# Queries made one group ahead, mixer sums and rotations on VectorE, and other rates for a background gather, in a two-layer diffusion backbone on one core

## Chip, cores and metric

One core of one Trainium2 chip. The metric is device time in microseconds (us) of one execution of the whole program: all work is one launch, with the inputs in the chip's main memory.

## What is computed

Two layers over 512 latent tokens and 256 context tokens of width 1024, all in float32. A layer first mixes tokens by three gated branches, then applies a retrieval of single-neuron experts:

```python
h = rms_norm(x) * (1 + scale1) + shift1
x += gate1 * W_out( sum_i sigmoid(h W_gate_i) * (branch_i(h) W_br_i) )
     # branches: windowed attention (8 heads, 2 kv heads, axial rotation, sinks, context keys),
     #           multi-scale pooling, chunked spatial gating
h = rms_norm(x) * (1 + scale2) + shift2
x += gate2 * peer(h)      # 8 heads, top 16 of 128*128 experts each: gelu(h . u_e) * softmax gate * v_e
```

The context tokens pass through layer 0 only (mixer and experts); layer 1 needs just their keys and values.

## The kernel before

The program runs in stages: the mixer of the context (0 to about 267 us), the mixer of the latent tokens in layer 0 (to about 785), the experts of layer 0 (`peer`, to about 2390), the latent mixer of layer 1 (to about 2835), the experts of layer 1 (to the end).

**Matmuls** are made in three passes (`mm3`, L217 to L223): weights and inputs are split into a rounded part and a remainder (`whi`, `wlo`), so every weight tile costs one load of 512 KB, one ScalarE copy (L189), one VectorE subtraction (L190) and 24 matmuls. `Weights.take` hands out such a tile in a fixed list order; each take is also a tick of `Background` (L48 to L79). A background job has a rate, and at every tick it makes that many steps.

**The experts of the latent tokens** are computed densely: for each of 128 tiles of u (L920 to L948) and then 128 tiles of v (L1060 to L1108), one take each. The selected gates are made by the job `front` on VectorE during the first 95 tiles.

**The 256 context tokens** find their experts' rows by gathering: for each of 2 blocks, 128 rows of u and then 128 rows of v per token. A step of the job `gather` (L804 to L829) issues one indirect transfer of 512 KB on POOL's queue (L801) into one of four buffers, two steps ahead, and consumes one on VectorE (L818 for u, L823 for v). These VectorE instructions keep their program order. 512 steps and 6 empty ones start in the layer-0 latent mixer (`gather_experts`, L1186) and end in the mixer of layer 1. The rates: 2.2 per take from the keys on (21 takes), 2.0 from the last branch on (16 takes) and in the output projection (8 takes), then by `peer`'s tuple 1.8 for the first 40 tiles of u, 1.4 for the next 55, 1.8 for the last 32; over v the rest is spread as `steps left / (128 + 8)` (L1038).

**A mixer** (`mixer`, L377) takes its weights in the order of `WS` (L394): spatial gating, keys, then per head group g its queries and two tiles of each of two output channels of the pooling branch, then the attention branch, then the output projection. `branch` (L482) makes, per output channel block o, a gate (`pj` to `th`, L491), the branch's product (`pb`), their product (`mt`, L501), and adds it to the sum `mg` (L502); the last branch also splits the sum into `mr` (L504) for the output projection (`pw_`, L673). The sum runs on POOL except for the last two blocks of the last branch. `rope` (L535) rotates keys and queries: a shuffle on VectorE, a multiplication by sin on POOL (L538), and two VectorE instructions.

The attention loop (L639) makes, per group, the queries (L640 to L645), then for each block b of 128 tokens the scores of both kv heads (`pc`, two buffers; maximum on VectorE L585, exponential on ScalarE L587) and the weighing of the block before (`weigh`: transposes L600, copies L602, products `po` L610). In group 0 two blocks of the pooling branch are made before the scores of b = 0; in groups 1 to 3 one before b = 0 and one before b = nb / 2.

Tile names: `g` gathered rows, `dots` and `hN` their results, `kT`, `qT`, `qs` keys and queries, `rs` the rotated copy, `wm` a job of layer 1's mixer that computes modulation vectors.

The framework orders each engine's instructions itself by a priority list, so moving a line in the code moves instructions on several engines.

Of the kernel before, what the change touches and what calls it, by code (L numbers as in the profile page):

```python
# [14 lines left out]
ALU = mybir.AluOpType  # L15
# [4 lines left out]
P = 128  # L20
# [62 lines left out]
def tile_backbone(ctx: ExitStack, tc: tile.TileContext, A, out):  # L83
# [5 lines left out]
    bg = Background()  # L89
# [287 lines left out]
    def mixer(l, x, r, lat, ps, start=None, settle=None, clear=None, after_attention=None, finish=None):  # L377
# [3 lines left out]
        with ExitStack() as es:  # L381
# [100 lines left out]
            def branch(br, wn, nk):  # L482
# [5 lines left out]
                for o in range(NCH):  # L488
# [8 lines left out]
                    if br == 2:  # L497
                        dve.scalar_tensor_tensor(mg[:, o], th, 1.0, pb, op0=ALU.add, op1=ALU.mult)
                    else:
                        t = pl.tile([P, T], F32, name="mt", tag="tt", bufs=3)  # L500
                        dve.scalar_tensor_tensor(t, th, 1.0, pb, op0=ALU.add, op1=ALU.mult)  # L501
                        (pool if br == 1 or o < 6 else dve).tensor_tensor(mg[:, o], mg[:, o], t, op=ALU.add)  # L502
                        if br == 0:
                            split(mr[0][o], mr[1][o], mg[:, o])  # L504
# [30 lines left out]
            def rope(t):  # L535
                s = pl.tile([P, T], F32, name="rs", tag="rs", bufs=2)
                dve.stream_shuffle(s, t, SHUF)
                pool.tensor_tensor(s, s, sin, op=ALU.mult)  # L538
                dve.tensor_tensor(t, t, cos, op=ALU.mult)
# [98 lines left out]
            last, ended = [], []  # L638
            for g in range(4):  # L639
                q = at.tile([P, T], F32, name="qT", tag="qT", bufs=2)  # L640
# [3 lines left out]
                qs2 = at.tile([P, 2, T], F32R, name="qs2", tag="qs2", bufs=2)  # L644
                split(qs2[:, 0], qs2[:, 1], q)  # L645
                finish_block()
                po = ps.tile([P, T], F32, name="po", tag="po", bufs=1)
                st = at.tile([P, 2, 2, nb], F32, name="st", tag="st", bufs=2)
                for b in range(nb):
                    for _ in range(2 * (b == 0) if g == 0 else b % (nb // 2) == 0):  # L650
                        next(second)
                    found = scores(qs2, st, g, b)
                    finish_group()
                    finish_block()
                    last.append((po, st, g, *found))
            finish_block()
            finish_group()
# [528 lines left out]
    def gather_experts():  # L1186
        bg.drain(jobs.pop())
        right.close()
        g4[0] = ctx.enter_context(tc.tile_pool(name="g4", bufs=1, side="right"))
        jobs.append(bg.add(gather(cblocks, 6), 2.2, 4 * P + 6))  # L1190

    def faster(pl, ps):
        jobs[0][1] = 2.0

    r = mixer(0, xT, rx[0], True, mps, start=find_experts, clear=gather_experts, after_attention=faster)
    eh.close()
    with tc.manual_schedule(engines={mybir.EngineType.Pool}):
        r = peer(0, r, (1.8, 1.4, 1.8, -8))

# [117 lines left out]
```

## Time and profile before

| | us |
|---|---|
| median of 3 runs (4096.03 to 4104.95) | 4099.12 |
| the profiled execution's own time | 4101.82 |
| its span, first to last instruction | 4100.0 |

PE is busy for 95% of the span, VectorE (DVE) for 77%, ScalarE (ACT) for 37%, POOL for 29%. A busy share averages over stages with different limits; a row of a window view gives the share of one stage.

### The profile page before, as it was taken

What the parts mean: (1) busy time and instruction counts of PE and PEld (TensorE: products, weight loads), DVE (VectorE), ACT (ScalarE), POOL (GpSimd) and SP (SyncE); (2) the same over time, 40 slices, a digit from 0 to 9 for tenths busy, and PEclk for the clock granted to TensorE, in tenths of its full rate; (3) what the DMA queues carried; (4) which work ended last, traced back from release to release, by engine and by line L of the source; (5) the groups of instructions that cost most, each with busy time, mean ns of one, the idle gap of its engine ahead of it and who ended that gap; (6) DMA issues with size and microseconds to landing.
All of it is one profiled execution on the core that took longest, in us unless ns stands there. A gap on an engine that the chain in (4) does not pass through costs nothing. (4 is left out here: it accounts for less than half of the span.)

```text
span 4100.0 us, 59061 instructions
## 1 busy us (share of the span) xinstructions
PE 3906.6 (95%) x21737; PEld 3391.9 (83%) x21737; DVE 3146.7 (77%) x6154; ACT 1498.7 (37%) x2320; POOL 1183.0 (29%) x942
## 2 busy tenths in 40 slices
PE   7999898899999999999999979999999999999998
PEld 5788776678778888788888867777889999999998
DVE  4569876799998876677778875645889986788887
ACT  3553343323344433222222233443234443333333
POOL 1111244411643324343333331110002224423331
PEclk9999999899999999999999989999999999999999
DMA  7753456655998998889999854323348999989996
GB/s 282 260 172 111 147 173 212 226 189 184 325 317 309 318 308 275 296 299 358 350 344 358 318 173 140 119 89 105 118 153 295 334 332 323 341 312 353 364 358 224
DMA packets 366099, 1051.86 MB, mean 257 GB/s; under 512 B 38384, under 2 KB 131312, under 8 KB 361200
## 3 DMA queue, kind: packets, MB, share of 16 engines
q1 hardware_dynamic: 170928, 544.18, 37.6%
q0 software_dynamic: 110592, 402.70, 28.5%
q10 hardware_dynamic: 84288, 101.20, 7.0%
q8 instruction: 170, 2.79, 0.3%
q14 instruction: 121, 0.99, 0.1%
HBM read 943.61 MB, written 104.33 MB: 256 GB/s over the span
## 5 line engine op out<-in xcount | busy, mean ns | idle before, releaser
L189 ACT CAST whi<-wraw 128x1024 fp32r<-128x1024 f32 (+2 forms) x756 | 752.6, 997 | 1672.2 <-issue 596.0
L190 DVE TENSOR_TENSOR wlo<-wraw,whi 128x1024 fp32r<-128x1024 f32 (+2 forms) x756 | 876.3, 1161 | 571.1 <-ACT whi L189 465.4
L801 POOL DMA_INDIRECT g<-in_u_dram,idx x384 | 500.9, 1304 | 1228.4 <-DVE dots L818 816.7
L801 POOL DMA_INDIRECT g<-in_v_dram,idx x384 | 511.8, 1333 | 913.3 <-DVE hN L823 845.5
L220 PE MATMUL pa<-h,whi 128*128 128x512 f32 (+1 forms) x2016 | 744.0, 369 | 2.5 <-ACT a L942 2.5
L1083 PE MATMUL acc<-ah,whi 128*128 128x512 f32 (+1 forms) x2048 | 740.4, 363 | 5.6 <-ACT ah L214 5.6
L1085 PE MATMUL acc<-ah,wlo 128*128 128x512 f32 (+1 forms) x2048 | 741.5, 362 | 0.0
L1084 PE MATMUL acc<-al,whi 128*128 128x512 f32 (+1 forms) x2048 | 741.4, 362 | 0.0
L221 PE MATMUL pa<-h,whi 128*128 128x512 f32 (+1 forms) x2016 | 734.4, 364 | 0.0
L818 DVE CUSTOM_DVE_ANT_0 g<-g,hN 128x1024 f32<-128x1024 f32 x384 | 466.2, 1236 | 50.5 <-DMA g<-in_u_dram,idx 50.4
L823 DVE SCALAR_TENSOR_TENSOR hN<-g,gate,hN 128x1024 f32<-128x1024 f32 x381 | 487.2, 1279 | 13.4 <-DMA g<-in_v_dram,idx 12.9
L223 PE MATMUL pa<-h,wlo 128*128 128x512 f32 (+1 forms) x2016 | 450.2, 364 | 2.9 <-DVE wlo L190 2.9
L1083 PEld LDWEIGHTS acc<-ah,whi 128*128 128x128 f32 x2048 | 384.7, 188 | 47.2 <-ACT ah L214 7.2
L1084 PEld LDWEIGHTS acc<-al,whi 128*128 128x128 f32 x2048 | 385.1, 188 | 40.4
L1085 PEld LDWEIGHTS acc<-ah,wlo 128*128 128x128 f32 x2048 | 385.0, 188 | 40.2
L220 PEld LDWEIGHTS pa<-h,whi 128*128 128x128 f32 x2016 | 381.1, 189 | 40.9 <-ACT a L942 2.8
L221 PEld LDWEIGHTS pa<-h,whi 128*128 128x128 f32 x2016 | 380.8, 189 | 38.2
L223 PEld LDWEIGHTS pa<-h,wlo 128*128 128x128 f32 x2016 | 368.5, 189 | 42.6 <-DVE wlo L190 3.2
L220 PE MATMUL pj<-h,whi 128*128 128x512 f32 (+1 forms) x792 | 288.9, 376 | 6.6 <-DVE nx L295 3.2
L221 PE MATMUL pj<-h,whi 128*128 128x512 f32 (+1 forms) x792 | 280.9, 366 | 1.3 <-POOL h L300 0.9
L942 ACT ACTIVATE a<-pa 128x512 f32<-128x512 f32 (+1 forms) x256 | 139.3, 546 | 271.1 <-PE pa L223 203.7
L220 PEld LDWEIGHTS pj<-h,whi 128*128 128x128 f32 x792 | 154.5, 195 | 46.8 <-issue 11.5
(527 smaller groups left out, 5428.2 us busy)
## 6 DMA issues: line engine op xcount, KB each, us to landing
wraw<-in_uT_dram SPq DMA_DIRECT2D x256, 512.0 KB, 5.3
wraw<-in_v_dram SPq DMA_DIRECT2D x256, 512.0 KB, 5.9
gd<-gs ACTq DMA_DIRECT2D x28, 2048.0 KB, 13.2
wraw<-in_winT_dram SPq DMA_DIRECT2D x100, 512.0 KB, 4.2
wm<-in_wmod_dram SPq DMA_DIRECT2D x64, 512.0 KB, 5.2
g<-gd SPq DMA_DIRECT2D x16, 2048.0 KB, 10.6
wraw<-in_wq_dram SPq DMA_DIRECT2D x48, 512.0 KB, 3.9
ad<-a ACTq DMA_DIRECT2D x96, 256.0 KB, 4.9
```

The costliest lines, as they stand in the source:

```text
L189: act.copy(hi, raw)
L190: dve.tensor_tensor(lo, raw, hi.bitcast(F32), op=ALU.subtract)
L220: pe.matmul(ps, wh[i], xh[i], start=i == 0, stop=False)
L221: pe.matmul(ps, wh[i], xl[i], start=False, stop=False)
L223: pe.matmul(ps, wl[i], xh[i], start=False, stop=i == n - 1)
L801: pool.indirect_dma_start(out=g, out_offset=None, in_=A[table], in_offset=bass.IndirectOffsetOnAxis(ap=idx, axis=0))
L818: ins = dve.tensor_tensor_reduce(out=g, in0=g, in1=hN, op0=ALU.mult, op1=ALU.add, scale=1.0, scalar=0.0, accum_out=dots[:, s:s + 1])
L823: ins = dve.scalar_tensor_tensor(hN, g, w, hN, op0=ALU.mult, op1=ALU.add)
L942: act.activation(a, pa[:, n_w:], AF.Gelu_apprx_tanh)
L1083: pe.matmul(acc[c], wh[:, s], ah, start=n == 0 and c % pair == 0, stop=False)
L1084: pe.matmul(acc[c], wh[:, s], al, start=False, stop=False)
L1085: pe.matmul(acc[c], wl[:, s], ah, start=False, stop=n == P - 1 and (c % pair == 1 or pair == 1 and not blocks))
```

## The change

Four edits. (1) The sums `mg` of all branches run on VectorE. (2) The sin product of `rope` runs on VectorE. (3) The queries of group g + 1 are made after the scores of block nb / 2 of group g, and group 0 has one block of the pooling branch before b = 0 and one before b = nb / 2, as the others. (4) The gather's rates fall from 2.2 to 1.0 and from 2.0 to 1.3 in the layer-0 mixer, and rise from 1.4 to 1.5 and from 1.8 to 2.3 in the second and third stretch of u.

```diff
-                        (pool if br == 1 or o < 6 else dve).tensor_tensor(mg[:, o], mg[:, o], t, op=ALU.add)
+                        dve.tensor_tensor(mg[:, o], mg[:, o], t, op=ALU.add)
...
                 dve.stream_shuffle(s, t, SHUF)
-                pool.tensor_tensor(s, s, sin, op=ALU.mult)
+                dve.tensor_tensor(s, s, sin, op=ALU.mult)
...
-            for g in range(4):
+            def queries():
                 q = at.tile([P, T], F32, name="qT", tag="qT", bufs=2)
                 act.mul(q, proj(ps, ws, hh, hl, T), 0.125)
                 if lat:
                     rope(q)
                 qs2 = at.tile([P, 2, T], F32R, name="qs2", tag="qs2", bufs=2)
                 split(qs2[:, 0], qs2[:, 1], q)
+                return qs2
+            coming = queries()
+            for g in range(4):
+                qs2 = coming
                 finish_block()
...
                 for b in range(nb):
-                    for _ in range(2 * (b == 0) if g == 0 else b % (nb // 2) == 0):
+                    if b % (nb // 2) == 0:
                         next(second)
                     found = scores(qs2, st, g, b)
                     finish_group()
                     finish_block()
                     last.append((po, st, g, *found))
+                    if b == nb // 2 and g < 3:
+                        coming = queries()
...
-        jobs.append(bg.add(gather(cblocks, 6), 2.2, 4 * P + 6))
+        jobs.append(bg.add(gather(cblocks, 6), 1.0, 4 * P + 6))
...
-        jobs[0][1] = 2.0
+        jobs[0][1] = 1.3
...
-        r = peer(0, r, (1.8, 1.4, 1.8, -8))
+        r = peer(0, r, (1.8, 1.5, 2.3, -8))
```

POOL in the last branch of the layer-0 latent mixer, before: `L801` issues an indirect transfer, `L502` is a sum.

```order
L801 DMA g_6732<-in_u_dram,idx 128x1024
L502 TENSOR_TENSOR mg<-mg,mt 128x512
L801 DMA g_6768<-in_u_dram,idx 128x1024
L801 DMA g_6771<-in_u_dram,idx 128x1024
L801 DMA g_6798<-in_u_dram,idx 128x1024
L801 DMA g_6801<-in_u_dram,idx 128x1024
L502 TENSOR_TENSOR mg<-mg,mt 128x512
L801 DMA g_6837<-in_u_dram,idx 128x1024
```

The same place of the changed kernel, where the indirect transfer is on line 809:

```order
L809 DMA g_6717<-in_u_dram,idx 128x1024
L809 DMA g_6753<-in_u_dram,idx 128x1024
L809 DMA g_6756<-in_u_dram,idx 128x1024
L809 DMA g_6783<-in_u_dram,idx 128x1024
L809 DMA g_6819<-in_u_dram,idx 128x1024
```

Four issues stood between two sums; now two or three fall to a channel block, and no sum stands among them.

VectorE in the layer-1 mixer, group 0, from the queries' remainder (`qs`) to the first score maxima (`mx<-pc`), before:

```order
L215 TENSOR_TENSOR qs_22680<-qT,qs_22680 128x512
L162 ISA wm,mod_80<-wm,silu,bm 128x1024
L162 ISA mod_80 128x1
L190 TENSOR_TENSOR wlo<-wraw,whi 128x1024
L501 SCALAR_TENSOR_TENSOR mt<-th,pb 128x512
L162 ISA wm,mod_80<-wm,silu,bm 128x1024
L162 ISA mod_80 128x1
L190 TENSOR_TENSOR wlo<-wraw,whi 128x256
...
L190 TENSOR_TENSOR wlo<-wraw,whi 128x1024
L501 SCALAR_TENSOR_TENSOR mt<-th,pb 128x512
L585 TENSOR_REDUCE mx<-pc 128x1 x2
```

And in the changed kernel:

```order
L215 TENSOR_TENSOR qs_22680<-qT,qs_22680 128x512
L162 ISA wm,mod_80<-wm,silu,bm 128x1024
L162 ISA mod_80 128x1
L501 SCALAR_TENSOR_TENSOR mt<-th,pb 128x512
L585 TENSOR_REDUCE mx<-pc 128x1
L502 TENSOR_TENSOR mg<-mg,mt 128x512
L586 TENSOR_TENSOR mx<-mx,nsk 128x1
L585 TENSOR_REDUCE mx<-pc 128x1
```

The second channel block of the pooling branch no longer stands ahead of the first maximum; a sum does.

VectorE in the same mixer at the end of group 0, changed kernel: the next group's rotation (`rs`, `qT`) among the maxima of the last block of scores. Before, it stood behind `L621` of this group.

```order
L537 STREAM_SHUFFLE rs<-qT 128x512
L585 TENSOR_REDUCE mx<-pc 128x1
L538 TENSOR_TENSOR rs<-rs,sin 128x512
L539 TENSOR_TENSOR qT<-qT,cos 128x512
L586 TENSOR_TENSOR mx<-mx,nsk 128x1
L585 TENSOR_REDUCE mx<-pc 128x1
L540 TENSOR_TENSOR qT<-qT,rs 128x512
L586 TENSOR_TENSOR mx<-mx,nsk 128x1
L215 TENSOR_TENSOR qs_22977<-qT,qs_22977 128x512
```

A maximum of the last block now waits behind up to three rotation instructions.

## Rows read from the trace of the kernel before

**Rows 1.** The page's head, its busy times, and the 40 slices of the span (102.5 us each): PE's and VectorE's busy tenths, the granted TensorE clock in tenths, and the data rate.

```profile
span 4100.0 us, 59061 instructions
PE 3906.6 (95%) x21737; PEld 3391.9 (83%) x21737; DVE 3146.7 (77%) x6154; ACT 1498.7 (37%) x2320; POOL 1183.0 (29%) x942
PE   7999898899999999999999979999999999999998
DVE  4569876799998876677778875645889986788887
PEclk9999999899999999999999989999999999999999
GB/s 282 260 172 111 147 173 212 226 189 184 325 317 309 318 308 275 296 299 358 350 344 358 318 173 140 119 89 105 118 153 295 334 332 323 341 312 353 364 358 224
```

**Rows 2.** The view of windows: stretch and its length in us, then the busy us (and instructions) of PE, of weight loads, of VectorE, ScalarE and POOL, the granted clock, the DMA share and GB/s. In order: attention of the layer-0 latent mixer, its last branch, the three stretches of u in layer 0, most of v in layer 0, attention of the layer-1 mixer, its last branch, and v in layer 1.

```profile
453.00:636.00 183.00, 163.60 (x1034) 130.45 (x1033) 133.50 (x229) 82.61 (x185) 73.18 (x56) 0.98 0.51 166
636.00:736.00 100.00, 76.66 (x298) 59.29 (x297) 62.05 (x97) 22.31 (x32) 54.15 (x38) 0.90 0.70 229
785.00:1118.00 333.00, 318.82 (x1587) 260.08 (x1586) 312.71 (x1084) 106.33 (x144) 107.26 (x67) 0.99 0.67 229
1118.00:1490.00 372.00, 369.81 (x2205) 303.90 (x2204) 323.94 (x420) 158.03 (x235) 141.02 (x85) 1.00 0.92 316
1490.00:1676.00 186.00, 185.31 (x830) 153.05 (x828) 108.83 (x129) 57.15 (x71) 71.86 (x57) 1.00 0.82 276
1800.00:2362.00 562.00, 562.00 (x2481) 465.35 (x2480) 448.74 (x536) 162.19 (x207) 192.85 (x168) 1.00 0.93 341
2532.00:2712.00 180.00, 166.01 (x1036) 132.79 (x1035) 114.97 (x199) 83.56 (x185) 23.23 (x13) 0.97 0.36 119
2712.00:2780.00 68.00, 68.00 (x297) 55.12 (x296) 28.16 (x36) 23.58 (x32) 9.76 (x6) 1.00 0.31 101
3700.00:4000.00 300.00, 300.00 (x1733) 300.00 (x1732) 250.50 (x299) 106.77 (x144) 95.50 (x80) 1.00 0.98 361
```

**Rows 3.** ScalarE's timeline (start us, length, instruction, idle before it and its releaser), the marks of both latent mixers: the keys, the first gate of the last branch, the first and the last of the eight squares that follow the output projection's channel blocks. Layer 0, then layer 1.

```profile
453.88 0.59 ACT L544 COPY kT<-pj 128x512 f32<-128x512 f32 x1 [0.76 <-PE pj L223]
636.72 0.60 ACT L491 ACTIVATE th<-pj 128x512 f32<-128x512 f32 x1 [0.76 <-PE pj L223]
736.31 0.63 ACT L253 ACTIVATE nsq<-xT 128x512 f32<-128x512 f32 x1 [3.11 <-DVE xT L674]
774.28 0.63 ACT L253 ACTIVATE nsq<-xT 128x512 f32<-128x512 f32 x1 [4.87 <-DVE xT L674]
...
2532.63 0.59 ACT L544 COPY kT<-pj 128x512 f32<-128x512 f32 x1 [0.76 <-PE pj L223]
2712.04 0.60 ACT L491 ACTIVATE th<-pj 128x512 f32<-128x512 f32 x1 [0.76 <-PE pj L223]
2780.01 0.63 ACT L253 ACTIVATE nsq<-xT 128x512 f32<-128x512 f32 x1 [1.55 <-DVE xT L674]
2817.93 0.63 ACT L253 ACTIVATE nsq<-xT 128x512 f32<-128x512 f32 x1 [4.87 <-DVE xT L674]
```

**Rows 4.** The view of waits, 650 to 785 us: engine and line waiting, what it waited for, us in total, times, the longest.

```profile
ACT mr L214 <- POOL mg L502: 42.7, 5, 10.9
DVE g L818 <- DMA g<-in_u_dram,idx: 32.3, 6, 7.1
PE pj L223 <- DVE wlo L190: 14.5, 5, 5.8
```

**Rows 5.** Groups of VectorE's and POOL's instructions by form in the last branch of layer 0's latent mixer, 636 to 736 us: count, busy us and mean ns, idle time before them and its releasers.

```profile
L818 DVE CUSTOM_DVE_ANT_0 g<-g,hN 128x1024 f32<-128x1024 f32 x31 | 37.8, 1254 | 32.3 <-DMA g<-in_u_dram,idx 32.3
L818 DVE DVE_READ_ACCUMULATOR2_ANT dots<- 128x1 f32 x31 | 2.5, 80 | 0.0
L502 DVE TENSOR_TENSOR mg<-mg,mt 128x512 f32<-128x512 f32 x2 | 1.4, 703 | 0.0
L801 POOL DMA_INDIRECT g<-in_u_dram,idx x32 | 46.8, 1464 | 54.3 <-DVE dots L818 49.4 <-issue 4.9
L502 POOL TENSOR_TENSOR mg<-mg,mt 128x512 f32<-128x512 f32 x6 | 8.1, 1358 | 1.7 <-DVE mt L501 1.6
```

**Rows 6.** DMA issues from 640 to 785 us: count and median us from issue to landing.

```profile
g<-in_u_dram,idx POOLq DMA_INDIRECT x42, 5.9
```

**Rows 7.** Waits of PE in the layer-1 mixer's attention (2532 to 2712 us).

```profile
PE pc L574 <- ACT s L587: 10.5, 4, 5.3
PE po L610 <- ACT sT L602: 1.9, 3, 1.5
```

**Rows 8.** The view of windows again, stretches of 6 us in the layer-1 mixer at the first scores of group 0 (two rows) and near that group's end.

```profile
2554.00:2560.00 6.00, 0.75 (x7) 0.54 (x5) 4.97 (x10) 3.27 (x6) 1.26 (x1) 0.85 0.90 302
2560.00:2566.00 6.00, 6.00 (x26) 5.85 (x26) 1.97 (x4) 2.90 (x9) 0.00 (x0) 0.58 0.10 35
2572.00:2578.00 6.00, 4.46 (x46) 3.47 (x44) 4.69 (x10) 3.15 (x9) 0.00 (x0) 1.00 0.11 34
```

**Rows 9.** One tile's instructions, the queries `qT`, over the whole span: count, min, median and max ns.

```profile
L539 DVE TENSOR_TENSOR qT<-qT,cos x8: 692/1764/1776, 463.8 to 2670.1; 128x512 f32<-128x512 f32 x8
```

**Rows 10.** Waits of PE in the context's mixer (0 to 267 us).

```profile
PE pc L574 <- ACT s L587: 2.9, 2, 2.3
```

**Rows 11.** The last stretch of u in layer 0 (1490 to 1676 us): the activations, one per tile of u, and the issues of the gather's transfers; count, min, median and max ns, first and last start.

```profile
L942 ACT ACTIVATE a<-pa x34: 592/598/603, 1494.8 to 1675.3; 128x512 f32<-128x512 f32 x34
L801 POOL DMA_INDIRECT g<-in_u_dram,idx x40: 933/941/1863, 1549.7 to 1667.2; - x40
```

## The prediction, on record before the changed kernel ran

> **What bounds the kernel now.** I read the page first [rows 1]: PE is busy for 3906.6 of 4100 us, so at most 193 us of idle time are to be had, and the tenths show where: the experts' stages stand at 9, the mixers (slices 1 to 8 and 24 to 27) at 7 to 9. Then the windows by stage [rows 2]. From 1118 to 2362 us PE waits for almost nothing (369.81 of 372, 185.31 of 186, 562 of 562), so no edit can gain there; it can only lose. From 636 to 736 us PE is busy for 76.66 of 100 us at a granted clock of 0.90, while the same code in layer 1 takes 68 us at 1.00 with PE full. In both attention stages PE idles: 183 - 163.6 = 19.4 us and 180 - 166 = 14.0 us.
>
> The marks on ScalarE give the stages their lengths [rows 3]. Last branch, from the first gate to the first square: 736.31 - 636.72 = 99.6 us in layer 0 against 2780.01 - 2712.04 = 68.0 in layer 1, which has no gather there. Keys to first gate: 182.8 against 179.4. The output projection, first square to last: 38.0 against 37.9, although layer 0 gathers two steps per take in it.
>
> So one stage loses 31.6 us to the gather. Its waits [rows 4] say how: VectorE stands 32.3 us waiting for gathered rows to land, PE 14.5 us for a `wlo` queued behind, ScalarE's `mr` 42.7 us for a sum on POOL. The groups of that stage [rows 5] close the account: VectorE's 62.05 busy us [rows 2] and its 32.3 us of waiting are 94.4 of the 99.6. VectorE sets the pace, and the rows that land late set VectorE's.
>
> **The change, part by part.** The sum is made against the profiled execution, 4101.8 us, which lies 2.7 us above the median of the runs.
>
> *Last branch of layer 0's mixer.* 16 takes at 1.3 make 20.8 steps where 2.0 made 32 (the rows show 31 in the window). Ten steps fewer free 10 x (1.254 + 0.080) = 13.3 us of VectorE; six sums moved there cost 6 x 0.703 = 4.2 [rows 5]. Its work becomes 62.05 - 13.3 + 4.2 = 53 us, under PE's 68. What matters is the landing. A buffer's round is an issue of 1.46, a landing of 5.9 [rows 6] and a use of 1.33: 8.7 us for four buffers. A channel block of two takes lasts 8.5 us at layer 1's pace; before, it asks for four rows, all buffers at once, and a sum of 1.36 us on POOL stands between the issues. After, it asks for 2.6, so a buffer has 13 us, and POOL's queue holds issues alone. If the waiting only shrank with the count (32.3 x 21 / 31 = 21.9), VectorE would need 75 us, a gain of 25; if the stage falls to PE's pace, 31.6; if all 32.3 us stayed, 85, a gain of 14. I take **28**, nearest to the output projection, which at 2.0 per take loses nothing [rows 3]. Ends: 14 and 32.
>
> *Attention, layer 1.* No gather runs there, so this is the order alone. The longest PE wait is 5.3 us for the exponentials of the first scores [rows 7]: VectorE has a whole pooling block in front of the first maximum. Behind it the clock stays low: 0.58 in the next 6 us and 0.85 in the wait itself [rows 8], that is 6 x 0.42 = 2.5 us of work at half of 2.4 GHz. With one block moved behind the scores of b = 1, the wait shrinks to about a maximum, an exponential and one sum, an estimated 1.5 us, and the clock need not fall: 3.8 + 2.5 = 6.3. The queries, 24 matmuls, now lie under the last block's softmax and cover the 1.5 us wait for `sT` near the end of group 0 [rows 7, 8]. Against that, the rotation stands among the maxima of the last block: up to three instructions of 0.7 (the minimum in [rows 9]), 2.1 us, covered by the transposes, products and the 5.5 us of the queries on PE; without that cover it would cost 2.1 us in three groups. I take **7**, ends -2 and 12 (of the 14 us idle and the 0.03 of 180 us that the clock lacks, some 19, a third must remain for softmax latencies).
>
> *Attention, layer 0.* The same 7, and the 3.4 us by which it is longer than layer 1's, since its steps fall from 46 to 21 in 21 takes: 25 x 1.33 = 33 us less on VectorE. I take **10**, ends 1 and 16.
>
> *Rotation and sums on VectorE elsewhere.* The multiplication by cos takes 0.692 at best and 1.764 in the median [rows 9]: beside POOL's multiplication it is held up by 1.07 us. So moving the product adds 0.69 us and takes away about as much. Attention holds 13 of these instructions, where VectorE is busy for 0.64 of layer 1's stage and 0.73 of layer 0's [rows 2]; I cost them at nothing, hidden by PE's matmuls, at the price of 13 x 0.7 = 9 us a mixer if VectorE were the bound.
>
> *Context mixer.* PE waits 2.9 us for exponentials [rows 10]; the order change can take part of it. Take **1**, ends -1 and 3. Its sums add 14 short instructions to a VectorE that is half idle.
>
> *What comes back in layer 0's experts.* By rates and takes, 94 steps less 6 empty ones stood before the experts; now 52 less 6 do. The 42 go to: 5 in tiles 41 to 95 (1.5 for 1.4), 17 in the last 32 tiles (2.3 for 1.8), 19 over v (1.75 for 1.60 per tile), 1 behind it. On VectorE 1.33 us each: in the second stretch 7 us beside 324 of 372, in the third 22 beside 109 of 186, over v 25 of 697 where 449 of 562 are busy [rows 2], all below PE. On the transfers: 0.15 x 524 KB per 5.44 us of v (24 matmuls; 2481 in 562 us) add 14 GB/s to 341, in the slices at 350 to 358 [rows 1] to some 367. The most that a row shows with PE full is 361, at a share of 0.98 [rows 2]. Four slices at 367 / 361 lose 7 us; none is lost if the transfers still have room. With some late rows I take a loss of **2**, ends 0 and 12.
>
> The Trainium skill (SBUF — State Buffer, section Summary: rules for kernel authors) plans transfers between main memory and SBUF at about 358 GB/s. By that figure four slices at 367 would stretch by 2.5%, an estimate of 10 us, and the sum below would be -36; the 361 GB/s with PE full speak for a ceiling a little higher, so I keep 2.
>
> **Sum:** -28 - 7 - 10 - 1 + 2 = -44. 4101.8 - 44 = 4058 for a profiled execution, 2.7 less for the median: **4055 us**.
>
> **Rivals.** *A. The queries' move only exchanges waits.* The maxima behind the rotation and the pooling blocks' `wlo` make PE wait as long as before; the attention terms shrink to the gather's 3. For it: VectorE is in order and fuller. Against: it is idle for a quarter to a third of those stages. 4099 - 28 - 3 - 1 + 2 = 4069.
>
> *B. The last branch stays bound by landings.* VectorE keeps its 32.3 us of waiting, since steps in program order still meet rows issued late; the gain is 14, the rest as forecast: 4069. Against it: a round of 8.7 us in 13. Both A and B: 4083.
>
> *C. v runs at the transfers' limit*: 10 us more, 4065.
>
> *D, slower: the gather's loop starves the last 32 tiles of u.* Four buffers set a pace. In the last branch four steps took 99.6 / 8 = 12.45 us, 3.11 each. If that is the loop's own pace, then 2.3 steps take 7.16 us, while a tile takes (1675.3 - 1494.8) / 33 = 5.47 [rows 11]; VectorE, in order, would hold `wlo`, and PE would lose 1.69 x 32 = 54 us: 4055 + 54 = 4109. It decides where a step costs over 5.47 / 2.3 = 2.38 us. Against it: the output projection took two steps in 37.97 / 7 = 5.42 us, 2.71 each, without loss; the round of 8.7 us gives 2.2. For it: the issue there takes 0.94 or, held up, 1.86 us [rows 11], and with 1.86 the round is 9.1, 2.27 a step, close to 2.38. Then half the stretch's idle VectorE time still lies between.
>
> The Trainium skill (SBUF — State Buffer, section SBUF: two separate sides) says that POOL cannot write a transfer's descriptors while VectorE runs an instruction that takes both shared ports. By that rule D is likelier, as the change puts more on VectorE and issues more there; the 1.86 beside 0.94 agree with it, and the median of 0.94 says that few issues are hit.
>
> **How the numbers follow.** About 0.2% (8 us) is what a measurement of this kernel can tell from no change. Forecast 64%, A 15%, B 8%, A and B 3%, C 5%, D 5%. D is the only case that ends slower. Tails of A with B and of the unknown ends land within 0.2% in about 5%. So faster 0.90, same 0.05, slower 0.05. The forecast's own ends: better terms (32, 12, 10, 1, 0) give 55, 4044; all best ends together 63, 4036. A, B and C lie up to 4069, A and B with a larger loss over v reach 4083 and more; 4080 leaves out that corner and D. Range 4036 to 4080.
>
> **What would show it.** Last branch of layer 0: first gate to first square 68 to 75 us, VectorE's wait for landings there under 10, `mr` no longer waiting for POOL. Keys to first gate about 172 us in both latent mixers, and no 6 us stretch with PE under 0.2 at group 0. The last stretch of u still with PE full at 2.3 steps per tile, and v at 5.44 us per tile with 355 GB/s. I am wrong if the last branch still takes over 85 us, if a wait of PE for `pc` of 5 us is still there in both layers, or if u's last tiles or v's take longer than 5.5 us.

## The result, and the profile after

| | before | after |
|---|---|---|
| median of 4 runs each (us) | 4097.89 | 4044.72 |
| lowest and highest of the changed kernel (us) | | 4040.54 to 4048.48 |
| ratio of the mean times, after to before, 95% interval | | 0.9867 [0.985, 0.9884] |
| the profiled executions' spans (us) | 4100.0 | 4040.8 |

The change takes 53 us off the median (1.3%) and 59.2 us off the profiled span; the forecast was 44. Single executions far slower than the others, one of `all_but_rates` and one of `v_heavy` below, are left out of medians and ratios. The marks on ScalarE, the same as in [rows 3], layer 0 and then layer 1 of the changed kernel (start, length, instruction, idle before it and its releaser):

```profile
445.80 0.59 ACT L544 COPY kT<-pj 128x512 f32<-128x512 f32 x1 [0.76 <-PE pj L223]
...
616.18 0.60 ACT L491 ACTIVATE th<-pj 128x512 f32<-128x512 f32 x1 [0.76 <-PE pj L223]
...
684.15 0.63 ACT L253 ACTIVATE nsq<-xT 128x512 f32<-128x512 f32 x1 [1.54 <-DVE xT L682]
...
2478.32 0.59 ACT L544 COPY kT<-pj 128x512 f32<-128x512 f32 x1 [0.76 <-PE pj L223]
...
2653.14 0.60 ACT L491 ACTIVATE th<-pj 128x512 f32<-128x512 f32 x1 [0.76 <-PE pj L223]
...
2721.11 0.63 ACT L253 ACTIVATE nsq<-xT 128x512 f32<-128x512 f32 x1 [1.54 <-DVE xT L682]
```

The differences between such marks, together with the last square of the context's mixer and the first and last activation of u, cut the whole span into stages. "Before, again" is a second profile of the kernel before, from another job; what it differs by from the first is the scatter of a stage.

| stage (us) | before | before, again | after | forecast of the difference | after less before |
|---|---|---|---|---|---|
| start to the context's keys | 113.9 | 113.0 | 115.0 | 0 | +1.1 |
| context's mixer, keys to last square | 148.6 | 145.3 | 142.7 | -1 | -5.9 |
| to layer 0's latent keys | 191.4 | 190.8 | 188.1 | 0 | -3.3 |
| attention, layer 0 | 182.8 | 182.3 | 170.4 | -10 | -12.4 |
| last branch, layer 0 | 99.6 | 97.1 | 68.0 | -28 | -31.6 |
| output projection and up to u | 64.6 | 64.4 | 64.6 | 0 | 0.0 |
| u, layer 0 | 874.4 | 881.0 | 873.7 | +2, with the next row | -0.7 |
| v and up to layer 1's keys | 857.3 | 854.3 | 855.8 | | -1.5 |
| attention, layer 1 | 179.4 | 179.2 | 174.8 | -7 | -4.6 |
| last branch, layer 1 | 68.0 | 68.0 | 68.0 | 0 | 0.0 |
| the rest | 1320.0 | 1317.2 | 1319.7 | 0 | -0.3 |

Three stages bring 48.6 of the 59.2. The windows by stage, which answer to [rows 2] (stretch, length; busy us and instructions of PE, weight loads, VectorE, ScalarE, POOL; granted clock, DMA share, GB/s): attention and last branch of layer 0, third stretch of u, most of v, attention of layer 1.

```profile
445.00:616.00 171.00, 160.38 (x1037) 129.57 (x1036) 101.78 (x188) 82.24 (x185) 15.96 (x17) 1.00 0.32 98
616.00:684.00 68.00, 68.00 (x296) 55.17 (x295) 53.56 (x81) 23.57 (x32) 23.01 (x19) 1.00 0.76 248
1430.00:1624.00 194.00, 192.81 (x874) 159.22 (x874) 139.01 (x134) 60.50 (x77) 102.22 (x76) 1.00 0.90 318
1748.00:2308.00 560.00, 560.00 (x2473) 463.68 (x2472) 466.05 (x570) 164.16 (x208) 215.35 (x184) 1.00 0.96 357
2478.00:2652.00 174.00, 161.84 (x1030) 131.07 (x1029) 115.98 (x212) 83.49 (x185) 0.00 (x0) 0.98 0.38 123
```

In the last branch of layer 0 PE is full at a granted clock of 1.00, and VectorE is busy for 53.56 us, where the forecast had worked out 53. The experts took the steps that went there with PE still full (560.00 of 560, 192.81 of 194), so nothing came back. Layer 1's attention has the clock still at 0.98 and 12 us of idle PE. Its first scores in stretches of 6 us, as in [rows 8]:

```profile
2490.00:2496.00 6.00, 2.59 (x17) 1.91 (x15) 6.00 (x12) 2.06 (x4) 0.00 (x0) 0.95 0.82 252
2496.00:2502.00 6.00, 5.28 (x21) 5.28 (x21) 3.92 (x9) 2.95 (x10) 0.00 (x0) 0.50 0.63 208
```

The hole at group 0 is smaller, but it is there, and behind it the clock is at 0.50, the level of 1.2 GHz. These stretches do not lie alike about the holes, so 0.50 cannot be set beside the 0.58 of before. Here are 12 us of each kernel, from 3 us before PE goes on after its wait, before and then after:

```profile
2557.00:2569.00 12.00, 9.11 (x52) 8.27 (x53) 4.93 (x11) 6.70 (x16) 0.67 (x1) 0.72 0.26 94
```
```profile
2494.00:2506.00 12.00, 9.28 (x49) 8.34 (x50) 7.27 (x16) 6.31 (x15) 0.00 (x0) 0.72 0.60 193
```

The granted clock is 0.72 in both, so the smaller hole has given back none of the clock there. PE's waits in layer 1's attention, as in [rows 7], show the hole as well, 3.8 us where it was 5.3:

```profile
PE pc L574 <- ACT s L587: 7.9, 4, 3.8
PE po L610 <- ACT sT L602: 2.4, 4, 0.7
```

The waits from 616 to 722 us, as in [rows 4]:

```profile
POOL g L809 <- DVE dots L826: 52.5, 17, 7.5
ACT mr L214 <- DVE mg L502: 18.3, 8, 2.4
```

VectorE's wait for rows that land, 32.3 us before, is gone from that list; POOL now waits for VectorE to hand a buffer back, so the gather is the one that waits. `mr` waits for VectorE's sum, 18.3 us where it was 42.7 for POOL's.

### The profile page after: what moved, and what is told of

The parts are those of the page before. It is cut to its first block, busy times and chain, and to the rows that moved or that the text cites. A ratio compares the mean times of both kernels' runs of the same rounds, so it can differ in the third digit from the quotient of the medians.

```text
span 4040.8 us, 59012 instructions
## 1 busy us (share of the span) xinstructions
PE 3885.5 (96%) x21737; PEld 3381.8 (84%) x21737; DVE 3157.0 (78%) x6206; ACT 1502.8 (37%) x2321; POOL 1064.5 (26%) x890
## 4 chain that ended last, share of the span: by engine, by line
PE 78%; DVE 11%; DMA 3%; issue 3%; ACT 2%; POOL 1%; ACTq 0%; DVEq 0%; POOLq 0%; SPq 0%
PE acc L1091 10%; PE acc L1093 10%; PE acc L1092 10%; PE pa L223 7%; PE pa L220 7%; PE pa L221 7%; PE pj L220 4%; PE pj L221 4%; PE pj L223 3%; DVE wlo L190 2%; DVE g L826 1%; PE pq L223 1%; DMA ad<-a 1%; PE pq L220 1%; PE pq L221 1%
## 5 line engine op out<-in xcount | busy, mean ns | idle before, releaser
L809 POOL DMA_INDIRECT g<-in_v_dram,idx x384 | 478.1, 1245 | 832.6 <-DVE hN L831 754.1
L826 DVE CUSTOM_DVE_ANT_0 g<-g,hN 128x1024 f32<-128x1024 f32 x384 | 463.6, 1222 | 53.6 <-DMA g<-in_u_dram,idx 53.5
```

Of the source, the lines that this page charges most:

```text
L809: pool.indirect_dma_start(out=g, out_offset=None, in_=A[table], in_offset=bass.IndirectOffsetOnAxis(ap=idx, axis=0))
L826: ins = dve.tensor_tensor_reduce(out=g, in0=g, in1=hN, op0=ALU.mult, op1=ALU.add, scale=1.0, scalar=0.0, accum_out=dots[:, s:s + 1])
```

## Experiments

Two questions were open: which of the four edits brought the 31.6 and 12.4 us of layer 0, and why layer 1 gave 4.6 and not 7. Two bounds of the forecast had also rested on estimates alone: the pace of the gather's loop (rival D) and the room that v has on the transfers (rival C).

**One edit at a time.** `rates_only` is the kernel before with edit (4), `sums_only` with (1), `rope_only` with (2), `queries_only` with (3); `all_but_rates` is the changed kernel with the old rates.

```diff
# rates_only
+        jobs.append(bg.add(gather(cblocks, 6), 1.0, 4 * P + 6))
...
+        jobs[0][1] = 1.3
...
+        r = peer(0, r, (1.8, 1.5, 2.3, -8))
# sums_only
+                        dve.tensor_tensor(mg[:, o], mg[:, o], t, op=ALU.add)
# rope_only
+                dve.tensor_tensor(s, s, sin, op=ALU.mult)
# all_but_rates, against the changed kernel
-        jobs.append(bg.add(gather(cblocks, 6), 1.0, 4 * P + 6))
+        jobs.append(bg.add(gather(cblocks, 6), 2.2, 4 * P + 6))
...
-        jobs[0][1] = 1.3
+        jobs[0][1] = 2.0
...
-        r = peer(0, r, (1.8, 1.5, 2.3, -8))
+        r = peer(0, r, (1.8, 1.4, 1.8, -8))
```

`queries_only` is the hunk on `queries()` and the attention loop, as the change has it.

> The kernel before with the gather's rates of the change alone. Theory T (the last branch of layer 0's latent mixer loses to rows that land late, because four of them are asked for per channel block): that stage falls from 99.6 us to 68 to 72 though its sums stay on POOL, attention of layer 0 from 182.8 to about 179.5, other stages within 2 us; the whole about 34 us less, 4064. Rival R (the sums on POOL between the issues are what delays the rows): the stage stays over 80 us, the whole at most 20 us less, 4078 or more.

> The kernel before with the sums on VectorE alone, the gather's rates as before. T: the last branch still asks for four rows per channel block, VectorE's wait for landings there stays over 20 us and the stage over 88 us; the whole 0 to 12 us less. R: the stage falls to 75 us or less and the wait for landings under 8 us; the whole about 25 us less.

> The kernel before with the rotation's sin product on VectorE alone. T: the product adds 0.69 us and the cos product falls from a median of 1.76 to 0.69 us, so VectorE's load and both attention stages stay within 2 us, the whole within 4 us of before. Rival (POOL's part of the rotation was on the way to the scores, 1.2 us of waiting per rotation and 1.1 us of held-up VectorE): each attention stage 4 to 8 us less, the whole 10 to 15 us less.

> The kernel before with the order of queries and pooling blocks alone. Theory: the order makes the gain in attention, so layer 1's stage falls from 179.4 to about 175, layer 0's from 182.8 to about 175 to 178, the context's mixer from keys to last square from 148.6 to about 143; the whole 13 to 18 us less. Rival (the gain in attention came from the instructions that left POOL): the stages move by under 2 us each, the whole by under 5 us.

> The changed kernel with the gather's rates of before: the other three edits together. If the edits in attention add up, layer 1's attention stays at 174 to 175 us as in the changed kernel, layer 0's, which keeps its 46 steps of the gather, lies at 174 to 178, the last branch of layer 0 at 88 to 95; the whole 15 to 20 us under before. Rival (each of the three only repeats the other's gain in attention): the whole 10 us or less under before.

| | median | ratio to before [95%] | attention, layer 0 | last branch, layer 0 | attention, layer 1 |
|---|---|---|---|---|---|
| before | | 1 | 182.8, 182.3 | 99.6, 97.1 | 179.4, 179.2 |
| `rates_only` | 4050.05 | 0.9898 [0.9872, 0.9925] | 172.5 | 68.0 | 178.9 |
| `sums_only` | 4083.94 | 0.9978 [0.9965, 0.9991] | 176.3 | 93.2 | 175.7 |
| `rope_only` | 4090.23 | 0.9991 [0.9979, 1.0004] | 181.5 | 98.6 | 175.8 |
| `queries_only` | 4085.75 | 0.9976 [0.9965, 0.9987] | 182.1 | 97.8 | 178.8 |
| `all_but_rates` | 4076.22 | 0.9967 [0.9954, 0.9981] | 171.9 | 93.5 | 174.1 |
| all four | 4044.72 | 0.9867 [0.985, 0.9884] | 170.4 | 68.0 | 174.8 |

Each ratio is to runs of the kernel before in the same job, so the ratios can be compared between jobs better than the medians.

Added up, the four edits alone would give 1.57% (1.02 for the rates, 0.55 for the three others). The change gives 1.33%, and the three others made together 0.33%. The intervals are too wide to say whether the gains add up; that the edits overlap shows in the stages.

Several expectations missed. `rates_only` took some 44 us off where 34 were expected, because layer 0's attention fell to 172.5 us and not to 179.5. `rope_only` was to leave both attention stages within 2 us, or by its rival to take 4 to 8 us off each: layer 1's lost 3.6, layer 0's 1.3. `queries_only` failed its theory in both attention stages and met it in the context's mixer (140.8 us); its whole, 8.5 us less by the medians, lies between theory and rival. `all_but_rates` took 12 us off where 15 to 20 were expected, although layer 0's attention fell below its range.

*Last branch:* the rates alone bring it to 68.0, with the sums still on POOL; the sums alone leave it at 93.2. The window of that stage and its two longest waits, in `rates_only`:

```profile
620.00:688.00 68.00, 68.00 (x297) 55.13 (x296) 56.37 (x76) 23.64 (x33) 35.02 (x26) 1.00 0.73 247
```
```profile
POOL g L801 <- DVE dots L818: 22.9, 15, 7.5
ACT mr L214 <- POOL mg L502: 17.1, 6, 2.9
```

and in `sums_only`, where the second and third are:

```profile
627.00:720.00 93.00, 74.35 (x295) 58.09 (x294) 64.98 (x102) 22.34 (x33) 45.13 (x31) 0.93 0.74 245
```
```profile
...
POOL g L801 <- DVE dots L818: 42.6, 15, 5.9
DVE g L818 <- DMA g<-in_u_dram,idx: 23.9, 6, 4.6
```

At the old rates 31 gathered rows fall into the stage, VectorE waits 23.9 us for them and PE loses the clock as well (0.93); at the new rates the wait is 0.4 us in `rates_only` and none in the changed kernel, whoever makes the sums. With the sums on VectorE alone the stage is 3.9 to 6.4 us shorter, by which of the two profiles of before it is held against; at the new rates they change nothing there.

*Attention of layer 0:* the windows of this stage in `queries_only` and in `all_but_rates`, beside [rows 2]:

```profile
442.00:624.00 182.00, 166.23 (x1033) 132.49 (x1032) 128.89 (x229) 82.18 (x185) 72.80 (x56) 0.97 0.51 165
```
```profile
444.00:615.00 171.00, 159.17 (x1030) 128.38 (x1029) 130.48 (x241) 81.86 (x184) 55.72 (x43) 1.00 0.55 176
```

The order alone does shorten PE's first wait here, from 5.7 to 2.5 us, and PE's idle time from 19.4 to 15.8; but PE is then busy for 2.6 us longer, at a granted clock of 0.97 for 0.98, and the stage gains only 0.7. The three edits without the rates bring the idle time to 11.8 us and the clock to 1.00, while VectorE stays as busy as before (130.5 us).

*Attention of layer 1:* the order of the queries, on which the 7 us had been put, gives 0.6 alone; the sums alone give 3.7 and the rotation alone 3.6, each about two thirds of what all three give (5.3). Both take work from POOL. The next rows are the multiplication by cos of that stage in the kernel before and in `rope_only` (count, min, median, max ns); the changed kernel's is as short, 684 to 689 ns:

```profile
L539 DVE TENSOR_TENSOR qT<-qT,cos x4: 692/1230/1775, 2542.7 to 2670.1; 128x512 f32<-128x512 f32 x4
```
```profile
L539 DVE TENSOR_TENSOR qT<-qT,cos x4: 683/684/689, 2534.1 to 2659.7; 128x512 f32<-128x512 f32 x4
```

POOL has nothing to compute there any more, and no product is held up. It is more than this one product: over layer 1's attention the busy times of VectorE's groups add up to 123.7 us (199 instructions) before and to 127.3 (212) after. Thirteen more at 0.685 us would have made 8.9; 5.3 us were given back by the others. The groups by form, 2533 to 2712 us of before and then 2478 to 2653 of after, show three that shrank:

```profile
L162 DVE CUSTOM_DVE_ANT_0 wm<-wm,silu,bm 128x1024 f32<-128x1024 f32 x29 | 37.9, 1321 | 0.0
...
L539 DVE TENSOR_TENSOR qT<-qT,cos 128x512 f32<-128x512 f32 x4 | 4.9, 1232 | 0.1
...
L190 DVE TENSOR_TENSOR wlo<-wraw,whi 128x256 fp32r<-128x256 f32 x8 | 4.5, 558 | 8.6 <-issue 8.6
...
L540 DVE TENSOR_TENSOR qT<-qT,rs 128x512 f32<-128x512 f32 x4 | 2.8, 692 | 2.6 <-POOL rs L538 2.4
```
```profile
L162 DVE CUSTOM_DVE_ANT_0 wm<-wm,silu,bm 128x1024 f32<-128x1024 f32 x29 | 36.6, 1278 | 0.0
...
L190 DVE TENSOR_TENSOR wlo<-wraw,whi 128x256 fp32r<-128x256 f32 x8 | 3.4, 421 | 14.6 <-issue 14.6
...
L539 DVE TENSOR_TENSOR qT<-qT,cos 128x512 f32<-128x512 f32 x4 | 2.7, 686 | 0.0
```

That is 1.3 + 2.2 + 1.1 = 4.6 us, and the wait of 2.4 us for POOL's product goes too. The Trainium skill (SBUF — State Buffer, section SBUF: two separate sides) says that the port which VectorE and POOL share is locked for a whole instruction by the one that starts first, not split; the rows agree: in the kernel before, the two products by cos that start after POOL's product take 1.77 us, and the two that start ahead of it 0.69. That these instructions shrank is measured; that they are what shortened the stage is argued, since VectorE is not full there and each wait of PE was not traced back to one of them. Part of the gain is the clock: with the sums alone PE's idle time in the stage falls by 1.6 us and its busy time by 2.1, with the rotation alone by 1.8 and 1.9. The kernel before has a second stretch at a low clock there, after a wait of PE of 2.0 us:

```profile
2640.00:2646.00 6.00, 6.00 (x40) 5.12 (x38) 4.05 (x8) 2.58 (x8) 0.00 (x0) 0.72 0.39 139
```

With either edit alone the clock is 1.00 from the end of the first such stretch to the last branch.

**The pace of the gather's loop, and the room over v.** Both are the changed kernel with another tuple of rates.

```diff
-        r = peer(0, r, (1.8, 1.5, 2.3, -8))
+        r = peer(0, r, (1.8, 1.5, 3.2, -8))   # last_u_32
+        r = peer(0, r, (1.8, 1.0, 1.5, -8))   # v_heavy and v_heavy_look
```

> The changed kernel with 3.2 instead of 2.3 gather steps per tile in the last 32 tiles of u: the slower rival of the prediction, provoked. If a step costs 2.2 us of a round of four buffers, a tile takes 7.0 us for 5.47 and the stretch 1430 to 1624 us lengthens by 40 to 50 us, with VectorE waiting for landed rows ahead of wlo. If a step costs 3.1 us, 140 us longer. If neither binds (PE stays full, VectorE waits under 40 us there), the rival had no ground at 2.3 either. v, with 1.54 steps per tile, unchanged within 2 us.

`last_u_32`: 4096.78, ratio 1.0021 [1.0009, 1.0032]. The stage of u grew from 873.7 to 917.5, 43.8 us, within the 40 to 50 expected. A tile of the last 32 then takes 5.47 + 43.8 / 32 = 6.84 us, 2.14 per step at 3.2. v, which was to stay within 2 us, took 7.9 us longer; why was not followed. Its third stretch, and the longest wait in it:

```profile
1426.00:1664.00 238.00, 205.48 (x869) 163.44 (x867) 165.49 (x180) 56.19 (x74) 138.32 (x101) 0.96 0.89 311
```
```profile
ACT whi L189 <- DMA wraw<-in_uT_dram: 100.3, 19, 8.5
```

ScalarE waits here for weight tiles, so the loop is not shown to be the only limit, and 2.14 is an upper bound of what the loop alone costs. 2.38 was the point from which rival D would decide, and 2.3 per tile at 2.14 is 4.92 of the 5.47 us. In the changed kernel VectorE waits for rows in that stretch as well (21.2 and 12.9 us), hidden under a full PE.

> The changed kernel with 1.0 and 1.5 steps per tile in the second and third stretch of u, so that 2.14 per tile are left for v, where 1.75 were. The transfers would need about 357 + 37 = 394 GB/s in v. If they end at 361 GB/s (the highest rate seen with PE full) or at 358, v takes 9% longer in its 96 tiles with reloaded activations, 40 to 50 us, and PE waits for weights or activations. If there is room up to 394, v stays at 703 us within 5 and the whole within 5 us of the changed kernel.

> The kernel v_heavy once more, for its stages: v of layer 0 at 2.14 gather steps per tile. By a ceiling of 361 GB/s v takes 40 to 50 us longer than 703 us and its window shows a DMA share of 0.97 or more at 355 to 365 GB/s with PE waiting; if the gather's loop is the limit (2.14 steps of 2.14 us are 4.6 of the 5.44 us of a tile) it is not reached. u stays at 871 to 874 us.

`v_heavy`: 4112.32, ratio 1.0054 [1.0033, 1.0075]. The rows are those of `v_heavy_look`, the same kernel again (4108.57, one run). v, from the last activation of u to its last matmul, takes 758.6 us against 705.0, 53.6 more than in the changed kernel where 40 to 50 were expected; 15 more are lost behind it, where the rest of the gather is. The middle of v, in the changed kernel and then in `v_heavy_look`:

```profile
1800.00:1880.00 80.00, 80.00 (x354) 66.25 (x353) 67.34 (x100) 23.81 (x30) 33.84 (x26) 1.00 0.97 366
...
1960.00:2040.00 80.00, 80.00 (x354) 66.24 (x354) 65.76 (x75) 23.14 (x30) 28.24 (x26) 1.00 0.97 370
```
```profile
1800.00:2280.00 480.00, 460.18 (x1958) 370.38 (x1957) 399.48 (x519) 131.29 (x164) 238.35 (x176) 0.98 0.98 368
2040.00:2120.00 80.00, 76.58 (x332) 61.56 (x331) 67.48 (x87) 22.84 (x29) 38.87 (x30) 1.00 1.00 378
```

0.39 steps more per tile ask for 0.39 x 524 KB / 5.44 us = 38 GB/s more. The rate stays where it was, 368 against 366 to 370, and the time gives. So the changed kernel's v, at 0.97 of the share with PE full, stands just under what the transfers give; 378 at a share of 1.00 is the most seen in these 80 us windows. That the transfers are the limit is read from rate and share; the loop alone needs at most 2.14 x 2.14 = 4.6 of the 5.44 us of a tile. VectorE and the loop wait for each other there too, so a part of theirs is not ruled out. Rival C was close, but it did not come.

**Why layer 1 gives less than layer 0.** With all edits layer 0's attention takes 170.4 us with its gather, layer 1's 174.8 without one. Group 0 of layer 1, ScalarE and then VectorE of the changed kernel (start, length, instruction):

```profile
2494.59 1.28 ACT L587 ACT_TABLE_LOAD   x1 [3.93 <-DVE mx L586]
2495.89 0.69 ACT L587 ACTIVATE s<-pc,mx 128x512 f32<-128x512 f32 x1
```
```profile
2491.36 1.27 DVE L162 CUSTOM_DVE_ANT_0 wm<-wm,silu,bm 128x1024 f32<-128x1024 f32 x1
...
2492.57 0.68 DVE L501 SCALAR_TENSOR_TENSOR mt<-th,pb 128x512 f32<-128x512 f32 x1
2493.16 0.68 DVE L585 TENSOR_REDUCE mx<-pc 128x1 f32<-128x512 f32 x1
```

Two things that layer 0 does not have stand in the chain from the first scores to the first exponential: a load of ScalarE's function table (1.28 us) and a piece of the job that computes modulation vectors (1.27). The load stood at this place in the kernel before, too:

```profile
2557.77 1.28 ACT L587 ACT_TABLE_LOAD   x1 [2.25 <-DVE mx L586]
```

`mods_rate_1` gives that job a rate of 1.0 for 1.5 and lets it end with the mixer; `exp_early` makes an exponential of eight numbers ahead of layer 1's keys, so that the table is loaded there; `exp_early_mods` does both.

```diff
# exp_early, where the sinks are read
+            if l == 1:
+                early = at.tile([P, 8], F32, name="early")
+                act.activation(early, sk, AF.Exp)
# mods_rate_1
-        jobs.append(bg.add(mod_rest(g4[0], "g4", NG4, silu, 1), 1.5))
+        jobs.append(bg.add(mod_rest(g4[0], "g4", NG4, silu, 1), 1.0))
...
-        r = mixer(1, xT, r, True, mps, start=second_context, settle=context_done, after_attention=all_mods)
+        r = mixer(1, xT, r, True, mps, start=second_context, settle=context_done, finish=all_mods)
```

> The changed kernel with the job of modulation vectors in layer 1's mixer (L162, 1.35 us each on VectorE) at 1.0 instead of 1.5 per take, so that it runs into the last branch, where VectorE is idle for half of the time. If these instructions in front of the score maxima keep the wait at group 0 (3.8 us, and the low clock behind it), layer 1's attention falls from 174.8 us towards layer 0's 170.4, to 170 to 172; the last branch stays at 68.0; the whole 3 to 5 us less. If not, attention stays at 174 to 175.

> The changed kernel with one exponential of 8 numbers more in layer 1's mixer, whose result nothing uses, so that ScalarE's table load of 1.28 us falls in the first branch and not between the first score maximum and its exponential. If that load keeps layer 1's first wait longer than layer 0's, PE's wait at group 0 falls from 3.8 to about 2.5 us; if the clock then stays up as in layer 0, layer 1's attention falls from 174.8 to about 171, else to 173.5. If the load is hidden anyway, attention stays within 0.5 us.

> The early exponential and the modulation job at 1.0 per take together. Layer 1's group 0 then has what layer 0's has, with one L162 (1.35 us) ahead of the first maximum: attention 170.5 to 172, the whole 3 to 5 us under the changed kernel. If the two do not add, attention stays at 173 to 174.

The table has the stage in three more profiles whose code in it is the changed kernel's; the clock is that of 12 us from 3 us before PE goes on after its wait at group 0.

| | median | ratio to before [95%] | attention, layer 1 | PE's wait at group 0 | granted clock |
|---|---|---|---|---|---|
| changed kernel | 4044.72 | 0.9867 [0.985, 0.9884] | 174.8 | 3.8 | 0.72 |
| same code, in `last_u_32` | | | 174.8 | 3.8 | 0.72 |
| same code, in `all_but_rates` | | | 174.1 | 3.8 | 0.86 |
| same code, in `v_heavy_look` | | | 173.9 | 3.8 | 0.86 |
| `mods_rate_1` | 4044.11 | 0.9891 [0.9868, 0.9915] | 173.9 | 4.2 | 0.86 |
| `exp_early` | 4042.05 | 0.9876 [0.9855, 0.9896] | 172.7 | 2.5 | 0.86 |
| `exp_early_mods` | 4042.05 | 0.9878 [0.9855, 0.9901] | 171.3 | 2.9 | 1.00 |

PE's wait at group 0 in `mods_rate_1`, `exp_early` and `exp_early_mods`:

```profile
PE pc L574 <- ACT s L587: 4.2, 1, 4.2
```
```profile
PE pc L577 <- ACT s L590: 2.5, 1, 2.5
```
```profile
PE pc L577 <- ACT s L590: 2.9, 1, 2.9
```

*The table load* is worth 1.3 us of this wait: without it 3.8 becomes 2.5, and 4.2 becomes 2.9. *The modulation piece* was not taken away. VectorE in `exp_early_mods`, ahead of the first maximum:

```profile
2496.70 1.28 DVE L162 CUSTOM_DVE_ANT_0 wm<-wm,silu,bm 128x1024 f32<-128x1024 f32 x1
...
2497.91 1.22 DVE L190 TENSOR_TENSOR wlo<-wraw,whi 128x1024 fp32r<-128x1024 f32 x1
...
2499.64 0.69 DVE L588 TENSOR_REDUCE mx<-pc 128x1 f32<-128x512 f32 x1
```

A piece still stands there, with a `wlo` behind it that stood ahead of the piece in the changed kernel, and at the lower rate the wait is 0.4 us longer. So what the piece costs is open. *The clock* does not follow from the wait alone. Here are the 12 us in `v_heavy_look`, whose wait is the changed kernel's, then in `exp_early_mods`, and then 12 us at the same place of layer 0 in `exp_early_mods`, where the code is the changed kernel's:

```profile
2558.00:2570.00 12.00, 8.82 (x51) 7.80 (x52) 7.73 (x17) 6.21 (x15) 0.00 (x0) 0.86 0.60 190
```
```profile
2499.00:2511.00 12.00, 9.08 (x60) 7.68 (x60) 7.38 (x16) 5.78 (x15) 0.00 (x0) 1.00 0.54 187
460.00:472.00 12.00, 9.61 (x54) 8.03 (x54) 3.64 (x9) 4.91 (x14) 0.00 (x0) 0.86 0.13 50
```

Behind the same wait of 3.8 us the clock reads 0.72 in two profiles and 0.86 in two, and the stage 174.8 against 173.9 to 174.1. A wait of 2.5 us reads 0.86 and one of 2.9 reads 1.00. Layer 0 has 1.00 in the changed kernel (170.4 us) and 0.86 with the same code here (171.9 us). So the 173.9 of `mods_rate_1` is within the scatter, and of the 171.3 of `exp_early_mods` only the shorter wait is shown to come from the edit; the 1.00 may be luck of one profile. In the whole kernel no version here is told apart from the changed one.

**The scatter of a stage.**

> The kernel before once more, for the spread of its stages. The start of layer 0's latent mixer, 191.4 us in the first profile and 187 to 189 in every other kernel, should read 187 to 189; the context's mixer from keys to last square should show whether 148.6 or the 145.7 of kernels that leave its order as it was is usual. Attention 182 to 183 and 179 us, last branch 98 to 100.

`before_again` (4094.42, one run) gives the third column of the stage table. It missed two of its expectations: the way to layer 0's latent keys took 190.8 us, and the last branch 97.1. The context's mixer, 5.9 us shorter after, is 3.3 us shorter there without any change. Over all profiles it takes 145.3 to 149.2 us in the five with the old order of the queries (mean 146.9), and 140.8 (`queries_only`) to 145.1 in the eight with the new one (mean 142.5). So the order gives about 4 us there. PE's wait for exponentials, 2.9 us in [rows 10], is 2.5 in `before_again` and not listed after; where the other 1.5 to 2 come from was not followed. The way from there to layer 0's latent keys takes 187 to 191 us: 188.1 in `rates_only` with the code of before (191.4 and 190.8), and 191.1 in `exp_early` with the code of after (188.1). The same code gives both ends, so the difference is taken as scatter.

## Why the prediction came out

**Last branch, layer 0: right, and near its best end.** Taken -28, measured -31.6 from the first profile of before and -29.1 from the second. The reading that VectorE's waiting for landings set the pace held, as did the 53 us of VectorE: fewer rows per block, and the wait went altogether instead of shrinking with the count. Rival B falls. The sum on POOL between the issues, one of two reasons given for it, was the smaller one.

**Attention, layer 0: right in sum, wrong in its split.** -12.4 for -10. The forecast had 7 for the order and 3.4 for the gather. The rates alone gave 10.3, the sums alone 6.5, and the order 0.7; the three edits other than the rates gave 10.9 together. The gains overlap, and a freer VectorE is not what they share: its busy time falls from 132.7 to 97.3 us with the rates alone and stays at 130.8 with the three others, and both bring the stage to 172 us. What they share is less idle time of PE (19.4 us before, 10.6 and 11.8) and the clock back at 1.00. Which waits gave way to which edit was not followed further.

**Attention, layer 1: the mechanism failed as the prediction put it.** The step "the wait shrinks to about a maximum, an exponential and one sum, an estimated 1.5 us, and the clock need not fall" did not happen: the wait went from 5.3 to 3.8 us, and the clock over the 12 us there stayed at 0.72. The estimate was low for its own terms: a maximum, an exponential and a sum take 0.68 or 0.69 us each in the changed kernel, 2.1 together. And two instructions of the chain were not counted, the table load in front of the first exponential and the modulation piece in front of the first maximum. The load is shown to cost 1.3 of the 3.8 us (`exp_early`); what the piece costs stays open. With the order alone this stage gains 0.6 us: PE's idle time in it even rises, from 14.0 to 15.4 us, and only its busy time falls.

The gain that there was came from the sums and the rotation, work that left POOL and that had been **costed at nothing**: each alone gives what the forecast did not have, 3.7 and 3.6 us. "Adds 0.69 us and takes away about as much" was right for one product, and it left out that sums on POOL hold up other VectorE instructions too. Rival A, in which the order only exchanges waits, describes layer 1 (0.6 us alone) better than the forecast does. In layer 0 the order did cut the first wait, from 5.7 to 2.5 us, but PE was busy for longer at a lower clock (0.97), and little of the gain was left. Rival A's time, 4069, did not come because the other edits paid.

That the two attention terms together came out at 17.0 us for a forecast of 17 is luck: 14 of the 17 were put on the order, which gives 1.3 us alone.

**Experts of layer 0: right.** A loss of 2 was taken; u and v together came out 2.2 us shorter, which is within the scatter of two profiles of before (874.4 and 881.0 for u). v kept PE full at 357 GB/s, where the text expected 355. By the 358 GB/s that the Trainium skill plans with (SBUF — State Buffer, section Summary: rules for kernel authors), v would have grown; the windows show 366 to 370 with PE full. The estimate of 2.2 us per step, which spoke against D, agrees with the bound of 2.14; the 3.11 read off the last branch was not the loop's own pace. The issues of the gather in the last tiles of u did get longer (median 1.0 to 1.5 us after for 0.94 before), and PE stayed full all the same.

**Context and start: too small.** -1 was taken for the context's mixer, with -3 as the best end; the means over the profiles differ by 4.4. The -3.3 up to the latent keys is scatter.

The sum of -44 was 15 short of the profiled difference and 9 short of that of the medians. Of the 15, 3.6 are the last branch, 2.4 layer 0's attention, 4.2 the experts, 8.2 the context's mixer and the way to the latent keys, against 2.4 too much in layer 1 and 1.1 at the very start.

## To carry to other kernels

When a background job shares an in-order engine with the foreground, find the stage in which that engine waits for the job's transfers, and move steps from there to a stage where the critical engine stays full; what the second stage can bear is read from the pace of one step and from the transfers' rate there, and both are worth a run of their own. Elementwise work taken from POOL can cost VectorE far less than its own duration, because VectorE stops being held up: here 8.9 us of instructions raised the sum of its busy times by 3.6. Before a wait is forecast to vanish, list every instruction in the chain that ends it, on each engine, a table load included. Before a change of the clock is put down to an edit, look at the same stretch in a second profile of the same code.

## What the runs showed of the hardware

- Transfers ran at 366 to 370 GB/s over 80 us windows with PE full, 378 at a share of 1.00; asking for 38 GB/s more changed the time, not the rate.
- One indirect transfer of 512 KB with four buffers costs at most 2.14 us per step when the loop is asked for more than it can give; an issue took from 0.93 to 1.99 us there.
- An `ACT_TABLE_LOAD` takes 1.28 us in the middle of a kernel too, and in front of an exponential that PE waits for it lengthens that wait by as much: 3.8 us with it, 2.5 without.
- The granted clock behind a wait of PE differs between profiles of the same code: over 12 us it was 0.72 twice and 0.86 twice behind a wait of 3.8 us, and the stage of 174 us differed by up to 0.9 us with it.
